# Token-major products of 512 columns in place of pairs of 256, and a ring of 11 small weight pieces in place of two whole blocks

## The chip, the cores and the metric

The kernel runs on one core of one Trainium2 chip. The metric is the device time of one execution in microseconds. Three runs of the kernel before gave 1104.18, 1104.21 and 1106.66 us; the profile was taken from a further execution of 1107.71 us.

## The reference, cut to what matters

Two layers of a streaming encoder over 1024 prompt positions and 8 x 16 sample frames, 1152 rows in all, with a model width of 1024. Per layer:

```python
h = x @ w_in                                   # 1024 -> 3072, split into eleven parts
uA, vA, zA, qB, fB, iB, zB, qC, kC, vC, zC = jnp.split(h, split_pts, axis=-1)
yA = sgu(uA, vA, ...) * silu(zA)               # chunked gMLP gating, mixer A
yB = hgrn2(silu(qB), 1 - f, iB, log f) * silu(zB)   # gated linear recurrence, mixer B
yC = window_attention(rope(qC), rope(kC), vC, sinks) * silu(zC)   # mixer C
out = layer_norm(alpha * x + concat(yA, yB, yC) @ w_out)          # 1024 -> 1024
```

All data is float32. The two large products, `x @ w_in` and `mix @ w_out`, are the bulk of the arithmetic.

## The kernel before, in words

The 1152 rows are nine tiles of 128. A group is three tiles (`GROUPS`); there are three groups per layer and six groups in all, numbered n = 0 to 5. Group n = 1 and n = 4 hold the sample tile.

**Split products.** Each float32 operand is split into a high and a low part (`wh` and `wl` for weights, `xh` and `xl` for the input, `mixh` and `mixl` for the mixers' output), and a product is the sum of three: high x high, low x high, high x low. `prod` issues 24 matmuls for it: eight slices of the depth times three kinds, one kind after the other. In `tok_major` the tile of 128 rows is the stationary operand and the weights stream, 256 columns at a time; in `feat_major` the weights are stationary and the 384 rows of a group stream.

**Weight blocks.** The weights come in blocks of 1024 x 256. A group uses 12 blocks of `w_in` and 4 of `w_out` (of the group before), in the order that the strings `P0`, `PN` and `PL` give; six of the twelve are token-major (K, Q0, Q1, I, ZB, V), as are O0 to O3, and the six others (F, Q, U, Z, C0, C1) are feature-major. A token-major block is three products, one for each tile; a feature-major one is two. Two blocks have room at a time (`wh` and `wl` with two buffers each). `next_w` hands out a block and at once issues the loads of the block after the next one to come.

**Raw and kept blocks.** A block that is used for the first time is loaded raw in four pieces of 256 KB through a staging ring (`wst`, four buffers), and each piece is split: ScalarE copies the high part, VectorE or GpSimd subtracts to get the low one. From the sixth block on (`NFIRST`) both parts are also written to DRAM, and later groups load them from there without splitting: two parts of 1 MB for a block, in DMAs of 512 KB. In group 0 and in group 3 most blocks are split; in group 1 the first five blocks of layer 0 are split again and kept this time, and so are the four of `w_out`.

**Lanes.** The mixers' own work (attention `lane_c`, recurrence `lane_b`, gating `lane_a`) is written as generators. `tick()` advances each of the three lanes by one step after every product; "+C", "+B", "+A" in a plan start a lane, "-C", "-X" and "-BX" run it out to its end. TensorE executes in the order of the program text; the order on the other engines and on SP's DMA queue is made by a list scheduler, in which weights have a high priority.

**Output.** `out_block` runs in the next group's plan, between attention's steps; `out_norm` does the layer norm of a tile after the last of its four blocks. `setup_out` loads the norm's weights once per layer into tiles of their own. After group 5 the four output blocks run with no lanes beside them.

The part of the plan of the middle groups that matters: `K Q0 Q1 -BX +C O0 O1 O2 O3 +X F Q U I +B ZB Z -C C0 C1 +N -X V +A`; of the last group: `K Q0 Q1 -BX +C O0 O1 O2 O3 +X U F Q I +B ZB Z -X V +A -C C0 C1`.

Of the kernel before, what the change touches and what calls it, by code (L numbers as in the profile page):

```python
# [25 lines left out]
TINY = float(2.0 ** -60)  # L26
NWST = 4
WDVE = ((1, 3), (1, 3))
NB1 = 3
NC4 = 3  # L30
PPT = 1
NEA = 3
NFIRST = 5
WDVE0 = (0, 1, 2, 3)
# [13 lines left out]
P0 = 'K Q0 Q1 -BX +C +X I F Q +B ZB U Z -C C0 C1 +N -X V +A'  # L48
PN = 'K Q0 Q1 -BX +C O0 O1 O2 O3 +X F Q U I +B ZB Z -C C0 C1 +N -X V +A'
PL = 'K Q0 Q1 -BX +C O0 O1 O2 O3 +X U F Q I +B ZB Z -X V +A -C C0 C1'  # L50
# [47 lines left out]
def body(ctx: ExitStack, tc: tile.TileContext, A, O, cst):  # L98
# [122 lines left out]
    def setup_out(l):  # L221
        d = lay[l]
        for n, k in (("ln_g", "lng"), ("ln_b", "lnb")):
            d[k] = T(k, [P, D], 1)
            nc.sync.dma_start(d[k], A[n][l].partition_broadcast(P))
# [10 lines left out]
    def setup_a(l):  # L236
        d = lay[l]
        for n, k in (("ln_v_g", "vg"), ("ln_v_b", "vb")):
            d[k] = T(k, [P, 256], 1)
            nc.sync.dma_start(d[k], A[n][l].partition_broadcast(P))  # L240
        d["bs"] = T("bs", [P, 2, P], 1)
        nc.sync.dma_start(d["bs"], A["bs"][l])
        rs = T("wst", [P, 4, 16], NWST)
        acquire("wst", NWST, nc.sync.dma_start(rs.rearrange("p g i -> p (g i)"), A["wss"][l].rearrange("j g i -> j (g i)").unsqueeze(0).to_broadcast([8, 16, 64])))
# [5 lines left out]
        up = tt(pool, wsS.rearrange("p g (c j) -> p g c j", c=8), rs.unsqueeze(2).to_broadcast([P, 4, 8, 16]),  # L250
                C("b8").unsqueeze(1).unsqueeze(3).to_broadcast([P, 4, 8, 16]), ALU.mult)
        release("wst", up)

    def plan(n):
        if n == 0:
# [4 lines left out]
    IN_COLS = {"K": 2304, "Q0": 1792, "Q1": 2048, "F": 1024, "Q": 768, "I": 1280, "ZB": 1536, "V": 256, "C0": 2560,  # L260
               "C1": 2816, "U": 0, "Z": 512}
    wlist = []
    for n, (l, g) in enumerate(order):
        for b in plan(n):
            if b in IN_COLS:
                wlist.append((l, "w_in", IN_COLS[b] // CB))
            elif b[0] == "O":
                wlist.append((order[n - 1][0], "w_out", int(b[1])))
    wlist += [(order[-1][0], "w_out", cb) for cb in range(4)]
    wq = []  # L270
    wpos = [0]
    kept = {}

    pieces = []

    def issue_w(off=WP):
        if wpos[0] >= len(wlist):
            return
        l, name, blk = wlist[wpos[0]]
        first = wpos[0]  # L280
        early = first if first < NEA else None
        eng_lo = WDVE0 if early is not None else WDVE[l]
        wpos[0] += 1
        key = (l, name, blk)
        with tc.high_priority(offset=off):
            wh, wl = T("wh", [P, 8, CB], 2, F32R), T("wl", [P, 8, CB], 2, F32R)
            if key in kept:
                for h in range(2):
                    ks = slice(4 * h, 4 * h + 4)
                    nc.sync.dma_start(wh[:, ks, :].bitcast(F32), kept[key][0][:, ks, :])  # L290
                    nc.sync.dma_start(wl[:, ks, :].bitcast(F32), kept[key][1][:, ks, :])
                wq.append((wh, wl))
                return
            keep = None
            if first >= NFIRST:
                nm = f"{name}{l}_{blk}"
                keep = kept[key] = [dp.tile([P, 8, CB], F32, tag=nm + c, name=nm + c) for c in "hl"]
            for kk in range(4):
                tag, bufs = ("wst", NWST) if early is None or kk == 3 else ("pT", 3) if early % 2 == 0 else ("c4", NC4)
                st = T(tag, [P, 2, CB], bufs)  # L300
                ld = nc.sync.dma_start(st, A[name][l, :, blk, 2 * kk:2 * kk + 2, :])

                def piece(kk=kk, st=st, tag=tag, bufs=bufs, ld=ld):
                    hw, lw = wh[:, 2 * kk:2 * kk + 2, :], wl[:, 2 * kk:2 * kk + 2, :]
                    with tc.high_priority(offset=WP):
                        copy(hw, st)
                        up = tt(dve if kk in eng_lo else pool, lw, st, hw.bitcast(F32), ALU.subtract)
                        if kk % 2 and keep:
                            ks = slice(2 * kk - 2, 2 * kk + 2)
                            nc.scalar.dma_start(keep[0][:, ks, :], wh[:, ks, :].bitcast(F32))  # L310
                            nc.sync.dma_start(keep[1][:, ks, :], wl[:, ks, :].bitcast(F32))
                    acquire(tag, bufs, ld)
                    release(tag, up)
                pieces.append(piece)
        wq.append((wh, wl))

    def do_pieces(k):
        for _ in range(min(k, len(pieces))):
            pieces.pop(0)()

    def next_w():
        do_pieces(99)
        w = wq.pop(0)
        issue_w()
        return w
# [24 lines left out]
    def tick():  # L350
        do_pieces(PPT)
# [3 lines left out]
    def prod(out, lh, ll, rh, rl, wmov, early=False):  # L355
# [4 lines left out]
        else:  # L360
            seq = [(ab, k) for ab in (hh, wh, wl) for k in range(8)]
        for n, ((a, b), k) in enumerate(seq):
            pe.matmul(out, a(k), b(k), start=n == 0, stop=n == 23)  # L363

    def tok_major(w, x, tt_, evac, early=False):
        ps = MM([P, CB])
        prod(ps, lambda k: x[0][:, k, tt_ * P:(tt_ + 1) * P], lambda k: x[1][:, k, tt_ * P:(tt_ + 1) * P],
             lambda k: w[0][:, k, :], lambda k: w[1][:, k, :], True, early)
# [3 lines left out]
    def feat_major(w, x, u, evac):  # L372
        ps = MM([P, 384])
        prod(ps, lambda k: w[0][:, k, u * P:(u + 1) * P], lambda k: w[1][:, k, u * P:(u + 1) * P],
             lambda k: x[0][:, k, :], lambda k: x[1][:, k, :], False)
# [499 lines left out]
    def out_block(op, cb):  # L875
        l, tiles = op["l"], op["tiles"]
        if cb == 0:
            if "lng" not in lay[l]:
                setup_out(l)
            op["ys"] = load_x(l, tiles)  # L880
            op["sts"] = [T("lst", [P, 4, 6], 3) for _ in tiles]
        ys, sts = op["ys"], op["sts"]
        w = next_w()
        cs = slice(cb * CB, (cb + 1) * CB)
        for tl, t in enumerate(tiles):
            def ev(ps):
                dve.scalar_tensor_tensor(ys[tl][:, cs], ys[tl][:, cs], ALPHA, ps, ALU.mult, ALU.add)
                dve.bn_stats(sts[tl][:, cb, :], ys[tl][:, cs])
                if cb == 3:
                    out_norm(l, t, ys[tl], sts[tl], LNM[op["n"]][tl])  # L890
            tok_major(w, mix, tl, ev)

    def out_norm(l, t, y, st, mode):
        d = lay[l]
# [3 lines left out]
        n = {"P": 0, "S": 768}.get(mode, D)  # L898
        if n < D:
            nb = T("sm", [P, 4], 12)  # L900
            dve.scalar_tensor_tensor(nb[:, 0:1], mv[:, 0:1], -1.0, mv[:, 2:3], ALU.mult, ALU.mult)
            z = y[:, n:]
            act.activation(z, z, AF.Identity, scale=mv[:, 2:3], bias=nb[:, 0:1])
            tt(pool, z, z, d["lng"][:, n:], ALU.mult)
            tt(pool, z, z, d["lnb"][:, n:], ALU.add)
        if n > 0:
            z = y[:, 0:n]
            dve.scalar_tensor_tensor(z, z, mv[:, 0:1], d["lng"][:, 0:n], ALU.subtract, ALU.mult)
            if mode == "A":
                act.activation(z, z, AF.Copy, scale=mv[:, 2:3])  # L910
                tt(pool, z, z, d["lnb"], ALU.add)
            else:
                dve.scalar_tensor_tensor(z, z, mv[:, 2:3], d["lnb"][:, 0:n], ALU.mult, ALU.add)
        if mode == "S":
            nc.sync.dma_start(yrows(l, t)[:, 0:n], y[:, 0:n])
            nc.sync.dma_start(yrows(l, t)[:, n:], y[:, n:])
        else:
# [10 lines left out]
    issue_w(2 * WP - 100)  # L928
    with tc.high_priority(offset=2 * WP - 200):
        xrs += load_xT(GROUPS[0][1:])  # L930
    pending, vlast = None, [None]

    def run_group(n, l, g, prev):
# [30 lines left out]
        def qc(qb):  # L964
            qks = G["qks"]
            w = next_w()
            for tl, t in enumerate(tiles):
                def ev(ps):
                    if t == "s":
                        copy(qks[tl][:, 0:8, :].rearrange("p (u r g) d -> p g r u d", u=2, g=2)[:, qb],  # L970
                             ps.rearrange("p (r u d) -> p r u d", r=2, u=2))
                    else:
                        copy(qks[tl][:, 4 * qb:4 * qb + 4, :], ps.rearrange("p (h d) -> p h d", h=4))
                    if qb == 1:
                        rope(l, t, qks[tl])
# [38 lines left out]
        def ib():  # L1014
            G["vts"] = [T("vt", [P, 2, 4, 64], 3) for _ in range(3)]
            w = next_w()
            for tl, t in enumerate(tiles):
                def ev(ps):
                    VS, v = G["vts"][tl], ps.rearrange("p (h v) -> p h v", h=4)
                    if t == "s":  # L1020
                        copy(VS[:, 0], v)
                    else:
                        copy(VS[0:64, 0], v[0:64])
                        copy(VS[64:128, 1], v[64:128])
                tok_major(w, x, tl, ev)
# [3 lines left out]

        def zb_():  # L1030
            w = next_w()
            zb = G["zb"]
            for tl in range(3):
                def ev(ps):
                    silu2(ps, 256, zb[:, tl, :])
                    z4 = zb[:, tl, :].rearrange("p (h v) -> p h v", h=4)
                    tt(eng("f"), z4, z4, d["ng"].unsqueeze(1).to_broadcast([P, 4, 64]), ALU.mult)
                tok_major(w, x, tl, ev)
# [126 lines left out]
```

## Time and profile before

| | |
|---|---|
| median of three runs | 1104.21 us |
| the profiled execution | 1107.71 us |
| its span, first to last instruction | 1105.6 us |
| TensorE busy with matmuls | 1069.6 us, 97% of the span |
| VectorE, ScalarE, GpSimd busy | 664.2, 513.2, 379.1 us |
| bytes moved by DMA | 269 MB, 243 GB/s on average |
| mean granted clock of TensorE | 0.989 of full speed |

Matmuls are pipelined: the duration shown of one is longer than the distance from one to the next, so the distance between the starts of rows in order of time is what a matmul costs. A row "x8" of the timeline merges eight instructions in a row.

### The profile page before, as it was taken

How to read it: one execution, taken by the hardware profiler on the slowest of the kernel's cores; microseconds unless marked ns; L12 is line 12 of the kernel's file. 1: busy time of each engine (PE TensorE's matmuls, PEld its weight loads, DVE VectorE, ACT ScalarE, POOL GpSimd, SP SyncE). 2: the span in 40 equal slices, each digit the busy share in tenths (PEclk: the TensorE clock that was granted, in tenths of full speed). 3: DMA queues.
4: the chain of work that ended last, by engine and by line, in shares of the span. 5: the costliest groups of instructions: out<-in, count | busy, mean ns of one | idle time of the engine just before them, and what ended most of it. 6: DMA issues, size and time to landing. Idle time of an engine off the chain costs nothing. (4 is left out here: it accounts for less than half of the span.)

```text
span 1105.6 us, 25914 instructions
## 1 busy us (share of the span) xinstructions
PE 1069.6 (97%) x10267; PEld 1003.1 (91%) x10267; DVE 664.2 (60%) x1714; ACT 513.2 (46%) x1297; POOL 379.1 (34%) x500
## 2 busy tenths in 40 slices
PE   9988999999999999999999998999999999999996
PEld 7977799998999999999999988999989999999996
DVE  4678654856374466277468678467536726746744
ACT  5687554655332376234257654345443324453310
POOL 3344375233224103384205465151405121123502
PEclk9998999999999999999999998999999999999999
DMA  9574589986558657656947987776856675576463
GB/s 323 186 260 160 185 307 357 307 314 249 181 202 295 217 184 270 226 196 242 345 181 266 349 306 278 274 256 243 297 189 204 216 269 197 186 280 218 161 224 134
DMA packets 88521, 269.07 MB, mean 243 GB/s; under 512 B 10448, under 2 KB 14032, under 8 KB 88400
## 3 DMA queue, kind: packets, MB, share of 16 engines
q1 hardware_dynamic: 79184, 233.86, 61.1%
q10 hardware_dynamic: 9216, 33.56, 7.9%
q8 instruction: 81, 1.33, 0.5%
q14 instruction: 40, 0.33, 0.1%
HBM read 188.73 MB, written 78.64 MB: 242 GB/s over the span
## 5 line engine op out<-in xcount | busy, mean ns | idle before, releaser
L143 POOL TENSOR_TENSOR wl<-wst,wh 128x512 fp32r<-128x512 f32 x68 | 97.8, 1449 | 200.2 <-ACT wh L126 129.4
L363 PE MATMUL mm<-wh,xh 128*128 128x256 f32 x864 | 128.4, 291 | 5.1 <-DVE t3k L383 2.6
L388 POOL TENSOR_TENSOR sm<-sm,ct 128x4 f32<-128x4 f32 (+2 forms) x42 | 47.9, 1141 | 225.3 <-DVE sm L387 225.3
L363 PE MATMUL mm<-wh,xl 128*128 128x256 f32 x864 | 123.3, 285 | 0.5 <-POOL xl L143 0.5
L363 PEld LDWEIGHTS mm<-wh,xh 128*128 128x128 f32 x864 | 111.8, 192 | 11.8 <-ACT wh L126 3.4
L363 PE MATMUL mm<-wl,xh 128*128 128x256 f32 x864 | 122.1, 284 | 0.0
L363 PE MATMUL mm<-xh,wh 128*128 128x384 f32 x576 | 121.2, 353 | 0.7 <-DVE t3k L383 0.7
L363 PEld LDWEIGHTS mm<-wh,xl 128*128 128x128 f32 x864 | 112.9, 194 | 0.7 <-POOL xl L143 0.7
L363 PE MATMUL mm<-xl,wh 128*128 128x384 f32 x576 | 112.5, 336 | 0.0
L363 PEld LDWEIGHTS mm<-wl,xh 128*128 128x128 f32 x864 | 112.4, 193 | 0.0
L363 PE MATMUL mm<-xh,wl 128*128 128x384 f32 x576 | 111.7, 335 | 0.0
L363 PEld LDWEIGHTS mm<-xh,wh 128*128 128x128 f32 x576 | 99.9, 192 | 4.8 <-issue 1.1
L126 ACT ACTIVATE wh<-wst 128x512 fp32r<-128x512 f32 x139 | 81.8, 625 | 44.2 <-DMA wst<-in_w_in 21.7
L363 PEld LDWEIGHTS mm<-xl,wh 128*128 128x128 f32 x576 | 102.2, 190 | 0.0
L143 DVE TENSOR_TENSOR wl<-wst,wh 128x512 fp32r<-128x512 f32 x71 | 70.9, 1007 | 51.1 <-ACT wh L126 46.2
L363 PEld LDWEIGHTS mm<-xh,wl 128*128 128x128 f32 x576 | 100.9, 188 | 0.0
L363 PE MATMUL mm<-wh,mixh 128*128 128x256 f32 x576 | 85.0, 290 | 1.5 <-ACT mixh L126 1.5
L363 PE MATMUL mm<-wh,mixl 128*128 128x256 f32 x576 | 80.8, 283 | 0.0
L363 PE MATMUL mm<-wl,mixh 128*128 128x256 f32 x576 | 80.8, 283 | 0.0
L477 ACT ACTIVATE c<-ax,sm 128x256 f32<-128x256 f32 (+1 forms) x128 | 57.2, 459 | 46.7 <-DVE sm L474 39.3
L363 PEld LDWEIGHTS mm<-wh,mixh 128*128 128x128 f32 x576 | 73.8, 191 | 1.7 <-ACT mixh L126 1.7
L363 PEld LDWEIGHTS mm<-wl,mixh 128*128 128x128 f32 x576 | 74.3, 192 | 0.0
(212 smaller groups left out, 1870.8 us busy)
## 6 DMA issues: line engine op xcount, KB each, us to landing
wst<-in_w_in SPq DMA_DIRECT2D x107, 256.0 KB, 5.5
xrow<-x SPq DMA_DIRECT2D x18, 512.0 KB, 4.5
wst<-in_w_out SPq DMA_DIRECT2D x32, 256.0 KB, 5.2
x<-xrow SPq DMA_DIRECT2D x9, 512.0 KB, 7.2
xrow<-in_xT SPq DMA_DIRECT2D x8, 512.0 KB, 6.7
xrow<-in_x_prompt SPq DMA_DIRECT2D x8, 512.0 KB, 6.0
wh<-w_in_3h SPq DMA_DIRECT2D x8, 512.0 KB, 5.5
wl<-w_in_3l SPq DMA_DIRECT2D x8, 512.0 KB, 7.9
```

The lines of the kernel that those rows point to most:

```text
L126: return act.activation(o, i, AF.Copy)
L143: return e.tensor_tensor(o, a, b, op=op)
L363: pe.matmul(out, a(k), b(k), start=n == 0, stop=n == 23)
L388: pool.tensor_tensor(out, out, mh[:, :out.shape[-1]], op=ALU.pow)
L477: acquire("c4", NC4, *[act.activation(pt[:, h, sl], pss[h // 2][:, h % 2, sl], AF.Exp, bias=nM[:, h:h + 1], scale=0.125, accum_out=rs[:, h ...
```

## The change

**Wide units.** Q0 and Q1 become one unit QC of 512 columns, I and ZB become IZ, and O0 to O3 become two units O0 and O1 of 512 columns. Their products stream 512 columns for each stationary tile. K, V and the feature-major blocks stay as they are. In a wide product there is a `tick()` after the twelfth matmul as well as at its end.

**Order in a product.** The three kinds now alternate for each slice of the depth, in place of one kind after the other.

**Ring.** The weights lie in 11 pieces (`NPC`) of [128, 2, 512]: 512 KB with both parts. A block of 256 columns is four pieces with two slices of the depth each, a wide unit eight pieces with one slice each. When the last product of a unit has made its last use of a piece, the piece is given back (`release`) and `pump` issues the next piece of the list. A kept piece is loaded by two DMAs of 256 KB. All raw pieces go through the four staging buffers; before, most of the first three blocks used other buffers too.

**Plan.** The lane of mixer B now starts after IZ, so ZB no longer stands behind its start.

**Norm.** The norm's weights are loaded for every group, in four tiles of 512 columns from the pool `t3k`, whose five buffers the recurrence's inputs use too. The norm works on halves of 512 columns; in mode "S" (the last group) VectorE does the first half and ScalarE and GpSimd the second, where the cut was at column 768 before.

```diff
+NPC = 11
-NEA = 3
-NFIRST = 5
+NEA = 2
+NFIRST = 4
-PN = 'K Q0 Q1 -BX +C O0 O1 O2 O3 +X F Q U I +B ZB Z -C C0 C1 +N -X V +A'
-PL = 'K Q0 Q1 -BX +C O0 O1 O2 O3 +X U F Q I +B ZB Z -X V +A -C C0 C1'
+PN = 'K QC -BX +C O0 O1 +X F Q IZ +B U Z -C C0 C1 +N -X V +A'
+PL = 'K QC -BX +C O0 O1 +X U F Q IZ +B Z -X V +A -C C0 C1'
...
     def setup_out(l):
-            d[k] = T(k, [P, D], 1)
-            nc.sync.dma_start(d[k], A[n][l].partition_broadcast(P))
+            for h in range(2):
+                r.append(T("t3k", [P, 512], 5))
+                nc.sync.dma_start(r[-1], A[n][l][512 * h:512 * h + 512].partition_broadcast(P))
...
+    def job(u, j):
+        l, name, i = wlist[u]
+        key = (l, name, i)
+        np_ = 4 if name == "w2" else 8
+        if j == 0 and key not in kept and u >= NFIRST:
+            nm = f"{name}{l}_{i}"
+            kept[key] = u, [dp.tile([P, np_, 512], F32, tag=nm + c, name=nm + c) for c in "hl"]
+        src, keep = kept.get(key, (u, None))
+        if src < u:
+            pc = T("w", [P, 2, 512], NPC, F32R)
+            acquire("w", NPC, *[nc.sync.dma_start(pc[:, c, :].bitcast(F32), keep[c][:, j, :]) for c in range(2)])
+        else:
+            st = T("wst", [P, 512], NWST)
+            raw = A[name][l, i].rearrange("p k c -> p (k c)")[:, 512 * j:512 * j + 512]
+            acquire("wst", NWST, nc.sync.dma_start(st, raw))
+            pc = T("w", [P, 2, 512], NPC, F32R)
+            hi = copy(pc[:, 0, :], st)
+            acquire("w", NPC, hi)
+            release("wst", tt(dve if u < NEA or j % 2 else pool, pc[:, 1, :], st, pc[:, 0, :].bitcast(F32), ALU.subtract))
+            if keep:
+                nc.scalar.dma_start(keep[0][:, j, :], pc[:, 0, :].bitcast(F32))
+                nc.sync.dma_start(keep[1][:, j, :], pc[:, 1, :].bitcast(F32))
...
+    def pump(off=WP, upto=1 << 30):
+        while jobs and jobs[0][0] < upto and rings["w"][0] - NPC < len(rings["w"][1]):
+            with tc.high_priority(offset=off):
+                job(*jobs.pop(0))
...
-            seq = [(ab, k) for ab in (hh, wh, wl) for k in range(8)]
+            seq = [(ab, k) for k in range(8) for ab in (hh, wh, wl)]
+        wide = out.shape[-1] == 512
         for n, ((a, b), k) in enumerate(seq):
-            pe.matmul(out, a(k), b(k), start=n == 0, stop=n == 23)
+            mm = pe.matmul(out, a(k), b(k), start=n == 0, stop=n == 23)
+            if per and n % (3 * per) == 3 * per - 1:
+                release("w", mm)
+                pump()
+            if wide and n == 11:
+                tick()
...
     def tok_major(w, x, tt_, evac, early=False):
-        ps = MM([P, CB])
+        n, per = 64 * len(w[0]), 8 // len(w[0]) if tt_ == 2 else None
+        ps = MM([P, n])
```

## Rows read from the trace of the kernel before

**Rows 1.** The page: busy time, and the span in 40 slices, in tenths.

```profile
PE 1069.6 (97%) x10267; PEld 1003.1 (91%) x10267; DVE 664.2 (60%) x1714; ACT 513.2 (46%) x1297; POOL 379.1 (34%) x500
...
PE   9988999999999999999999998999999999999996
...
DMA  9574589986558657656947987776856675576463
```

**Rows 2.** Groups by line and shape, TensorE: count, busy us, mean ns, idle before.

```profile
L363 PE MATMUL mm<-wh,xh 128*128 128x256 f32 x864 | 128.4, 291 | 5.1 <-DVE t3k L383 2.6 <-ACT wh L126 1.9 <-ACT vt L126 0.5
...
L363 PE MATMUL mm<-xh,wh 128*128 128x384 f32 x576 | 121.2, 353 | 0.7 <-DVE t3k L383 0.7
...
L363 PE MATMUL mm<-wh,mixh 128*128 128x256 f32 x576 | 85.0, 290 | 1.5 <-ACT mixh L126 1.5
```

**Rows 3.** Timeline of TensorE, in two stretches of uninterrupted products: start, duration.

```profile
239.71 1.55 PE L363 MATMUL mm<-xh,wh 128*128 128x384 f32 x8
...
242.48 1.55 PE L363 MATMUL mm<-xh,wl 128*128 128x384 f32 x8
...
1084.33 1.12 PE L363 MATMUL mm<-wh,mixh 128*128 128x256 f32 x8
...
1094.89 1.12 PE L363 MATMUL mm<-wl,mixh 128*128 128x256 f32 x8
```

**Rows 4.** Timeline of the TensorE end of group 5: lane B's last steps, first output product.

```profile
1048.58 0.69 PE L829 MATMUL ax<-vt,AQ 128*64 128x64 f32 x16
...
1059.34 0.38 PE L845 MATMUL ax<-idn,t1b 128*128 128x128 f32 x2
...
1062.03 0.39 PE L363 MATMUL mm<-wh,mixh 128*128 128x256 f32 x1 [1.48 <-ACT mixh L126]
```

**Rows 5.** Timeline of all engines: a step of lane B, first and last instruction.

```profile
1033.38 0.69 PE L829 MATMUL ax<-vt,AQ 128*64 128x64 f32 x16
...
1038.74 0.42 DVE L143 TENSOR_TENSOR t1b<-ax,t1b 128x256 f32<-128x256 f32 x1
```

**Rows 6.** Stages: PE, PEld, DVE, ACT, POOL busy (count), clock, DMA share, GB/s.

```profile
155.00:254.00 99.00, 97.51 (x770) 92.96 (x768) 60.59 (x128) 54.31 (x127) 43.49 (x46) 1.00 0.93 328
...
390.00:400.00 10.00, 10.00 (x87) 9.91 (x86) 5.85 (x17) 7.66 (x24) 0.00 (x0) 1.00 0.59 209
590.00:690.00 100.00, 94.17 (x926) 86.42 (x928) 74.85 (x173) 59.07 (x127) 53.37 (x62) 0.97 0.88 314
205.00:235.00 30.00, 30.00 (x250) 27.89 (x249) 24.02 (x53) 18.76 (x54) 8.48 (x6) 1.00 0.81 276
```

**Rows 7.** Timeline of SP's queue, group 2: a kept block's four loads.

```profile
381.98 0.79 SPq L290 DMA_DIRECT2D wh<-w_out_2h  x2
382.94 0.79 SPq L291 DMA_DIRECT2D wl<-w_out_2l  x2
```

**Rows 8.** DMA issues: count, KB each, median us from issue to landing.

```profile
wst<-in_w_in SPq DMA_DIRECT2D x107, 256.0 KB, 5.5
...
wl<-w_out_2l SPq DMA_DIRECT2D x8, 512.0 KB, 7.0
```

**Rows 9.** Groups by line and shape: the splitting of one raw piece.

```profile
L143 POOL TENSOR_TENSOR wl<-wst,wh 128x512 fp32r<-128x512 f32 x68 | 97.8, 1449 | 200.2 <-ACT wh L126 129.4 <-PE mm L363 35.6 <-DVE lst L888 8.4
...
L126 ACT ACTIVATE wh<-wst 128x512 fp32r<-128x512 f32 x139 | 81.8, 625 | 44.2 <-DMA wst<-in_w_in 21.7 <-PE mm L363 13.6 <-DMA wst<-in_w_out 4.1
...
L143 DVE TENSOR_TENSOR wl<-wst,wh 128x512 fp32r<-128x512 f32 x71 | 70.9, 1007 | 51.1 <-ACT wh L126 46.2 <-PE mm L363 3.5 <-POOL X L143 1.1
```

**Rows 10.** Timeline of all engines: the end of the last tile's norm.

```profile
1097.79 0.42 DVE L888 BATCH_NORM_STATS2 lst<-xrow 128x6 f32<-128x256 f32 x1
...
1102.25 0.72 POOL L143 TENSOR_TENSOR xrow<-xrow,lnb 128x256 f32<-128x256 f32 x1
1103.00 0.33 SPq L916 DMA_DIRECT2D out_y_prompt<-xrow  x1
```

**Rows 11.** Timeline of TensorE at the start: first product of the second block.

```profile
18.02 1.21 PE L363 MATMUL mm<-wh,xh 128*128 128x256 f32 x8
```

More of the change, by code (lines that the diff above doesn't have):

```diff
@@ L264, in body @@
         for b in plan(n):
[L265 to L271, printed above, removed]
-    kept = {}
[L274 to L315, printed above, removed]
@@ L317, in do_pieces @@
-    def do_pieces(k):
-        for _ in range(min(k, len(pieces))):
-            pieces.pop(0)()
+            if b in UNITS:
+                wlist.append((order[n - 1][0] if b[0] == "O" else l, *UNITS[b]))
+    wlist += [(order[-1][0], "wo", cb) for cb in range(2)]
+    kept = {}
+    units = [([], []) for _ in wlist]
+    jobs = [(u, j) for u, (_, name, _) in enumerate(wlist) for j in range(4 if name == "w2" else 8)]
+    rings["w"] = [0, []]
+    ucur = [0]
+    def job(u, j):
[20 more added lines that the diff above has]
+                nc.sync.dma_start(keep[1][:, j, :], pc[:, 1, :].bitcast(F32))
+        units[u][0].append(pc[:, 0, :])
+        units[u][1].append(pc[:, 1, :])
@@ L373, in feat_major @@
         ps = MM([P, 384])
-        prod(ps, lambda k: w[0][:, k, u * P:(u + 1) * P], lambda k: w[1][:, k, u * P:(u + 1) * P],
-             lambda k: x[0][:, k, :], lambda k: x[1][:, k, :], False)
+        prod(ps, wcols(w[0], u * P, (u + 1) * P), wcols(w[1], u * P, (u + 1) * P),
+             lambda k: x[0][:, k, :], lambda k: x[1][:, k, :], False, per=2 if u == 1 else None)
         evac(ps)
@@ L877, in out_block @@
         if cb == 0:
-            if "lng" not in lay[l]:
-                setup_out(l)
+            op["ln"] = setup_out(l)
             op["ys"] = load_x(l, tiles)
-            op["sts"] = [T("lst", [P, 4, 6], 3) for _ in tiles]
+            op["sts"] = [T("lst", [P, 2, 6], 3) for _ in tiles]
         ys, sts = op["ys"], op["sts"]
         w = next_w()
-        cs = slice(cb * CB, (cb + 1) * CB)
+        cs = slice(512 * cb, 512 * cb + 512)
         for tl, t in enumerate(tiles):
@@ L897, in out_norm @@
         rstd(mv[:, 2:3], mv[:, 1:2], LN_EPS)
-        n = {"P": 0, "S": 768}.get(mode, D)
-        if n < D:
+        if mode in "PS":
             nb = T("sm", [P, 4], 12)
             dve.scalar_tensor_tensor(nb[:, 0:1], mv[:, 0:1], -1.0, mv[:, 2:3], ALU.mult, ALU.mult)
[L902 to L911, printed above, removed]
-            else:
[L913 to L917, printed above, removed]
+        for h in range(2):
+            g, b, z = ln[0][h], ln[1][h], y[:, 512 * h:512 * h + 512]
+            if mode == "P" or mode == "S" and h == 1:
+                act.activation(z, z, AF.Identity, scale=mv[:, 2:3], bias=nb[:, 0:1])
+                tt(pool, z, z, g, ALU.mult)
+                tt(pool, z, z, b, ALU.add)
+            else:
+                dve.scalar_tensor_tensor(z, z, mv[:, 0:1], g, ALU.subtract, ALU.mult)
+                if mode == "A":
+                    act.activation(z, z, AF.Copy, scale=mv[:, 2:3])
+                    tt(pool, z, z, b, ALU.add)
+                else:
+                    dve.scalar_tensor_tensor(z, z, mv[:, 2:3], b, ALU.mult, ALU.add)
+            if mode == "S":
+                nc.sync.dma_start(yrows(l, t)[:, 512 * h:512 * h + 512], z)
+        if mode != "S":
             nc.sync.dma_start(yrows(l, t), y)
@@ L962, in kv, with qc @@
                 params()
-        def qc(qb):
+        def qc():
             qks = G["qks"]
@@ L1100, in run_group @@
                 "-BX": lambda: drain("B", "X")}
-        for i in range(4):
+        for i in range(2):
             acts[f"O{i}"] = lambda i=i: out_block(prev, i)
@@ L1110, in body @@
     drain("B", "X")
-    for cb in range(4):
+    for cb in range(2):
         out_block(pending, cb)
@@ L1122, in _layout @@
     xs, xp = i["x_sample"].reshape(1, 128, 8, 128), i["x_prompt"].reshape(8, 128, 8, 128)
-    blocks = lambda w: w.reshape(2, 8, 128, -1, CB).transpose(0, 2, 3, 1, 4)
+    cols = lambda w, at, n: np.stack([w.reshape(2, 8, 128, -1)[..., c:c + n] for c in at], 1).transpose(0, 1, 3, 2, 4)
     rows = lambda v: np.broadcast_to(v.reshape(1, -1), (128, v.size))
```

82 lines of the change are left out of this document (39 added, 43 removed).

## The prediction

> **What bounds the kernel now.** I read the busy times first: TensorE has matmuls in flight for 97% of the span, the others far less, and the row of 40 slices is full but for three 8s, the start and the end [rows 1]. So a change of TensorE's own instructions shows in the time, and whatever makes TensorE wait adds to it. But "busy" says nothing of what a matmul costs, since neighbours overlap. I therefore went to the timeline for the distance between starts. With 256 columns, 11 rows of 8 matmuls lie between the starts at 1084.33 and 1094.89: 10.56 us / 88 = 120.0 ns. With 384 columns, two rows of 8 between 239.71 and 242.48: 2.77 us / 16 = 173.1 ns [rows 3]. 128 columns more cost 53.1 ns, which is 2.41 GHz; the rest, 120.0 - 106.2 = 13.8 ns, is paid once per matmul whatever its width. The groups by shape give the counts: three kinds of 864 and three of 576 with 256 columns, 4320 in all, and 1728 with 384 [rows 2]. 4320 x 120.0 + 1728 x 173.1 ns = 817 us, so three quarters of the span are large products. Then the stages: in two long ones, 155 to 254 us (group 1, where weights are split and kept) and 590 to 690 us (group 3), the DMA engines are 93% and 88% busy; elsewhere, as at 390 to 400 us, 59% [rows 6]. DMA is the second thing near its limit, and only there: 328 / 0.93 = 353 GB/s at full load.
>
> **The change, part by part.**
>
> *Width.* Of the 4320 matmuls of 256 columns, those of K and V (2 blocks x 3 tiles x 24 x 6 groups = 864) stay; the 3456 of Q0, Q1, I, ZB and O0 to O3 become 1728 of 512. The trace has none of 512. The lower bound is the line through the two widths: 120.0 + 2 x 53.1 = 226.2 ns. The upper bound is 240.0, two of 256 with nothing saved. I take the line, since 384 columns lie on it together with 256 and nothing in the rows bends there. Gain: 1728 x 13.8 ns = 23.8 us, bounds 0 and 23.8. The stationary operand is loaded before every matmul as now, and the new order within a product changes neither count nor width: 0.
>
> A page speaks against this. The Trainium skill, "TensorE: Matmul & The Clock Gate", section on the back-to-back issue gap, gives N / 2.4 GHz plus about 2.5 ns per matmul, so that a pair would save 2.5 ns: an estimate of 4.3 us in all. The distance of 120.0 ns at 256 columns does not agree with the 109.2 that this gives; I go by the row.
>
> *Steps of the lanes.* A group had 42 ticks: 30 token-major products and 12 feature-major ones. It still has 42: K and V give 6, four wide units of three products give 24, the feature-major ones 12. Twelve wide matmuls last 2.71 us where 24 narrow ones lasted 2.88, so a lane has 0.17 us less between steps: 0, for the slack that TensorE's full row shows, at most some 3 us.
>
> *End of the last group.* Here order costs. Lane B needs twelve steps. Before, ZB, Z, V, C0 and C1 give 12 ticks after its start, and its twelfth step (the transposes at 1059.34) falls on the last tick [rows 4]. Now only Z, V, C0 and C1 follow: 9. Steps 10 to 12 run with no product between them, and TensorE, in order, waits. Step 10's chain, from the matmuls at 1033.38 to the end of the last product on VectorE at 1039.16, took 5.8 us among other work [rows 5], and before it stands the state's update of step 9, which I estimate at a fifth of that, 1.2 us. Against it goes the 1.48 us that the first output product waits now [rows 4], which will be over by then. Upper bound 5.8 + 1.2 - 1.5 = 5.5; lower bound 0, if VectorE and GpSimd have everything ready. I take +3.5, nearer to the row.
>
> *Ring.* In a wide unit 8 of 11 pieces are held, so three of the next unit lie ready. A wide product lasts 24 x 226.2 ns = 5.43 us and uses a piece for 0.68. Piece i is given back 0.68 x (i + 1) us into the last product; its place goes to piece i + 3 of the next unit. If that is wide too, piece 7 is needed 5.43 + 7 x 0.68 = 10.2 us after the last product's start, some 0.7 more with a lane step between. Five pieces, 2.6 MB, have to come in that time. *Kept:* a block's four loads of 512 KB start at 381.98, the last issue is at about 383.4, and it lands 7.0 us later: 2.1 MB in 8.4 us [rows 7, 8]. Half a MB more at 353 GB/s is 1.5 us: 9.9 after the first give-back at 0.68, 10.6 against 10.9. It just fits, and only where nothing else is in the queue. *Raw:* ScalarE needs 0.63 us a piece, VectorE 1.01 or GpSimd 1.45 in turn [rows 9]; four pieces wait in staging, the fifth is loaded after the first is split (0.68 + 0.63 + 1.01), lands 5.5 us later [rows 8] and is split by 9.5. It fits if VectorE is free, but in the output stage of group 1 VectorE is busy 24.0 of 30 us [rows 6]. Wide follows wide at QC to O0 and O0 to O1 in groups 1 to 5, and at the last O0 to O1: 11 times, 7 of them into kept and 4 into raw pieces. Everywhere else a narrow unit stands on one side, with 7 pieces ahead or four uses of 1.04 us and more: 0. For the 7 I take 0.3 us each (0 to 1), for the 4 I take 1 us each (0 to 3): +6, bounds 0 and 19. Behind a late weight load on SP's queue stand only further loads, which are less urgent.
>
> *DMA.* The norm's weights are loaded 24 times 256 KB, before 4 times 512: +4.2 MB, of which 1.05 fall on group 1. In the stage at 93% this costs up to 1.05 MB / 353 GB/s = 3.0 us; and its three wide pairs (QC, O0, O1: 3 x 72 x 13.8 ns = 3.0 us) save nothing if DMA sets the pace. Group 3's stage has two such pairs, 2.0 us. Bounds 0 and 8; I take half, +4. More and smaller DMAs: a pair of issues takes 0.79 us [rows 7], a wide piece needs one pair per 0.68 us in a burst of five, which the moving of the bytes outlasts: 0.
>
> *Norm and tail.* The last matmul ends at 1094.89 + 1.12 = 1096.0, the last statistics at 1098.2, the last issue is at 1103.0 [rows 3, 10]. With a wide last product VectorE has the tile before behind it: two instructions of 512 columns, at most twice 0.42 us each, end 1.7 us after the matmul, not 2.2. GpSimd's two instructions double from 0.72 us to at most 1.44, ScalarE's grows some 0.2: -0.5 + 1.4 + 0.2, +1 rounded, bounds 0 and 2.
>
> *Start.* The second unit's first product begins at 18.02 [rows 11] and its eight pieces now pass four staging buffers. Piece loads follow the splitting of K's pieces, in two rounds of about 7 us (5.5 to land, 0.63 and 1.01 to split) from 7 us on: all there by some 21, needed from 18.0 to 22.8. 0, at most +3.
>
> Sum: -23.8 + 3.5 + 6 + 4 + 1 = -9.3 us. The profiled execution took 1107.7 us for a span of 1105.6, so 1098.4 for its like; it lay 3.5 us above the median, and against the median, 1104.2, the forecast is 1095.
>
> **Rivals.** *The ring is ample*, and DMA hides: for it speaks that TensorE hardly waits for weights today, 1.9 us of idle in the largest group [rows 2], and that 11 pieces are more than the 8 of before. Then 1104.2 - 23.8 + 3.5 + 1 = 1085. *Starvation at wide after wide*: the same arithmetic with 0.3 us of slack at its thinnest. Without the ring's term the sum is -15.3 us, so it decides from 15.3 / 11 = 1.4 us per passage on; at 2.5 us, what one norm load of 1 MB in front costs, it gives 1104.2 - 15.3 + 27.5 = 1116. *VectorE and lanes set the pace* where it is 75 to 80% busy [rows 6]: of the 24 pairs half save nothing, -11.9 + 14.5, 1107. *Width saves nothing*, because a product's fixed part grows with the columns: two widths on one line speak against it; 1104.2 + 14.5 = 1119. By the page's rule it would be 1114; the trace gives that little chance.
>
> **How the numbers follow.** Forecast 0.50 (1088 to 1101), ample ring 0.20 (1080 to 1088), VectorE and lanes 0.11, starvation 0.14, no gain of width 0.05. A measurement of this kernel tells from no change what is over about 0.3%, 3.3 us. Faster takes the first two, 0.70; the third lies within and takes 0.02 of starvation's mild cases, 0.13; slower 0.17. The range runs from 1081, nearly the whole gain of width, to 1112, into starvation; the forecast's own is 1088 to 1101.
>
> **What the profile would show.** Distances of 226 ns between wide matmuls, 8539 matmuls in place of 10267. In group 5 a gap of some 4 us on TensorE between the last product of C1 and the first of O0, ended by the transposes of line 845's like. Small waits for weights at the first product of O0 and O1, in groups 1 and 4 for ScalarE or VectorE, else for DMA. DMA near full in groups 1 and 3. The prediction is wrong if wide matmuls lie 240 ns apart, if the waits for weights at the 11 passages sum to well over 6 us or are missing, or if TensorE's idle time grows in stages without wide units.

## The result, and the profile after

The changed kernel took 1135.45 us (median of 4 runs, 1132.46 to 1139.28): 1.0283 times the kernel before, interval 1.0246 to 1.0320. The forecast was 1095 with a range up to 1112; the kernel became slower, by 31 us. The profiled execution took 1132.46 us for a span of 1130.7.

The page, busy times and slices, as in [rows 1]:

```profile
PE 1067.7 (94%) x8539; PEld 914.2 (81%) x8539; DVE 647.8 (57%) x1666; ACT 517.0 (46%) x1287; POOL 375.9 (33%) x506
...
PE   7969999899999999999999898999999999999986
...
PEclk9979999999999999999999999999999999999989
```

The 1728 matmuls fewer are there, but TensorE's idle time rose from 1105.6 - 1069.6 = 36 us to 1130.7 - 1067.7 = 63 us, and holes and a lower clock show at the start. A measurement of one kernel spreads by some microseconds: the interval above is worth 4 us to each side. So a difference between two edited kernels below is uncertain by some 2 to 7 us.

First, what the width gave: the timeline of TensorE in the last output unit, to compare with [rows 3].

```profile
1095.97 0.61 PE L345 MATMUL mm<-w,mixh 128*128 128x512 f32 x2
...
1106.17 0.62 PE L345 MATMUL mm<-w,mixh 128*128 128x512 f32 x2
```

Between these two starts lie 45 matmuls, three for each 0.68 us: 10.20 us / 45 = 226.7 ns, where the line through the two narrower widths gave 226.2. So 1728 x (240.0 - 226.7) = 23.0 us were saved, as forecast, and about 54 us were lost elsewhere. Where TensorE waits for a result of another engine or for a DMA, by the view of waits (engine, tile and line that wait, releaser: us in total, times, longest):

```profile
PE ax L456 <- DVE qT L145: 10.1, 6, 2.4
PE mm L345 <- DVE t3k L376: 7.5, 2, 5.0
PE mm L345 <- ACT w L128: 5.9, 4, 2.8
PE ax L822 <- POOL vt L741: 5.5, 4, 2.6
PE ax L581 <- DVE c L145: 4.5, 2, 2.3
PE ax L838 <- DVE t1b L145: 4.2, 2, 3.3
PE ax L797 <- DMA X<-in_st: 4.2, 2, 2.8
...
PE mm L345 <- DMA w<-wo_1h: 1.1, 3, 0.8
```

The `ax` rows are steps of lanes B and C, the `mm` rows products. A ring that starves TensorE would fill rows like the last; together with two smaller ones of its kind it comes to 1.6 us. Most of the waits are the lanes' (L456 and L581 are lane C, L797, L822 and L838 lane B). Those on `ACT w` are the start. The row on `t3k` is the first product of IZ, which waits for VectorE's work on Q, 5.0 us in group 0 and 2.5 in group 3; the kernel before had 3.3 us of such waits.

The last group, end of lane B, in TensorE's timeline, as in [rows 4] (L822 and L838 are L829 and L845 there; a bracket is the idle time in front and its releaser):

```profile
1060.04 0.33 PE L822 MATMUL ax<-vt,AQ 128*64 128x64 f32 x2
1063.02 0.85 PE L822 MATMUL ax<-vt,AQ 128*64 128x64 f32 x13 [2.65 <-POOL vt L741]
...
1065.43 0.84 PE L345 MATMUL mm<-xh,w 128*128 128x384 f32 x2
1066.07 0.52 PE L345 MATMUL mm<-xl,w 128*128 128x384 f32 x1
1066.39 0.84 PE L345 MATMUL mm<-xh,w 128*128 128x384 f32 x2
...
1080.54 0.91 PE L822 MATMUL ax<-vt,AQ 128*64 128x64 f32 x14 [1.63 <-POOL vt L741]
1084.73 0.69 PE L838 MATMUL ax<-idn,t1b 128*128 128x128 f32 x2 [3.28 <-DVE t1b L145]
...
1085.64 0.63 PE L345 MATMUL mm<-w,mixl 128*128 128x512 f32 x1
...
1086.92 0.63 PE L345 MATMUL mm<-w,mixl 128*128 128x512 f32 x1
```

Three waits, 7.6 us, on a chain that had none in [rows 4] but the 1.48 at its end; and products that run slowly behind them. The windows say why (start:end, length, busy of PE, PEld, DVE, ACT, POOL, granted clock, DMA share, GB/s):

```profile
1045.30:1060.00 14.70, 14.70 (x204) 13.47 (x199) 12.45 (x38) 3.65 (x7) 10.61 (x18) 1.00 0.42 144
...
1064.50:1068.00 3.50, 3.50 (x12) 3.38 (x12) 2.87 (x9) 1.58 (x4) 0.61 (x2) 0.53 0.92 289
...
1081.40:1088.20 6.80, 3.52 (x11) 2.80 (x10) 1.95 (x6) 0.77 (x2) 1.01 (x1) 0.50 0.23 84
```

By the waits of 2.65 and 3.28 us lie stretches at half the clock, 1.2 GHz: the first begins 1.4 us behind its wait, the second takes its wait in. So a wait can cost more than its own length: O0's first matmuls take nearly twice their time. The mean granted clock of the whole span was 0.989 before and 0.978 after; with a low level of 0.5 that is 2 x 0.011 x 1105.6 = 24 us at half clock before, and 2 x 0.022 x 1130.7 = 50 after.

### The profile page after: what moved, and what is told of

The parts are those of the page before. It is cut to its first block, busy times and chain, and to the rows that moved or that the text cites. A ratio compares the mean times of both kernels' runs of the same rounds, so it can differ in the third digit from the quotient of the medians.

```text
span 1130.7 us, 23131 instructions
## 1 busy us (share of the span) xinstructions
PE 1067.7 (94%) x8539; PEld 914.2 (81%) x8539; DVE 647.8 (57%) x1666; ACT 517.0 (46%) x1287; POOL 375.9 (33%) x506
## 4 chain that ended last, share of the span: by engine, by line
PE 65%; DVE 11%; DMA 9%; issue 6%; ACT 5%; POOL 5%; ACTq 0%; SPq 0%; POOLq 0%; DVEq 0%
PE mm L345 50%; DMA wst<-in_w 4%; PE ax L494 2%; PE ax L456 2%; PE ax L485 2%; DVE W L145 1%; POOL X L145 1%; PE ax L570 1%; DVE X L145 1%; ACT w L128 1%; DVE w L145 1%; DMA X<-in_st 1%; DMA wst<-in_wo 1%; POOL w L145 1%; PE ax L855 1%
## 5 line engine op out<-in xcount | busy, mean ns | idle before, releaser
L345 PE MATMUL mm<-w,xh 128*128 128x256 f32 (+1 forms) x1152 | 306.9, 350 | 13.7 <-DVE t3k L376 7.5
L345 PE MATMUL mm<-xh,w 128*128 128x384 f32 x1152 | 313.0, 343 | 0.9 <-DVE tanh L376 0.8
L345 PEld LDWEIGHTS mm<-w,xh 128*128 128x128 f32 x1152 | 205.6, 196 | 45.3 <-DVE t3k L376 8.0
L345 PEld LDWEIGHTS mm<-xh,w 128*128 128x128 f32 x1152 | 212.5, 190 | 4.5 <-ACT t3k L128 1.2
L345 PE MATMUL mm<-w,xl 128*128 128x256 f32 (+1 forms) x576 | 197.7, 345 | 0.0
L345 PE MATMUL mm<-w,mixh 128*128 128x512 f32 x576 | 195.8, 404 | 1.7 <-DMA w<-wo_1h 1.1
L345 PE MATMUL mm<-xl,w 128*128 128x384 f32 x576 | 194.9, 338 | 0.0
L345 PEld LDWEIGHTS mm<-w,xl 128*128 128x128 f32 x576 | 112.6, 196 | 10.7
L345 PE MATMUL mm<-w,mixl 128*128 128x512 f32 x288 | 112.9, 392 | 0.0
L345 PEld LDWEIGHTS mm<-xl,w 128*128 128x128 f32 x576 | 109.8, 191 | 0.2
L456 PE MATMUL ax<-kT,qT 128*128 128x256 f32 (+1 forms) x256 | 42.9, 301 | 10.5 <-DVE qT L145 10.1
```

The source lines that it names most:

```text
L345: mm = pe.matmul(out, a(k), b(k), start=n == 0, stop=n == 23)
L456: pe.matmul(ps[:, hh, sl], qT[:, hh, 2 * g + j, :], kk, start=hh + c == 0, stop=False)
```

## The experiments

Ratios are to the kernel before, run on the same chip beside each. Theory 1, formed from the rows above: the order of the stages, in which lane B starts later and, in groups 1 to 4, U comes later (the section on the change names only the first; the diff has both), leaves lane steps at places where TensorE must wait for them. Rival: the ring.

### The order of the stages

**Lane B late, in the kernel before.**

```diff
-... I +B ZB ...
+... I ZB +B ...
```

> The kernel before with one edit: lane B starts behind ZB, three ticks later, as far as the changed kernel moved it. Theory 1: this edit alone costs a good part of what the changed kernel lost in the lanes, 1114 to 1130. The prediction's own figure for the last group, 3.5 us, would give 1107 to 1108. Rival (ring starvation, which this kernel cannot have): 1104 to 1108.

Measured: 1132.26 us, 1.0247 [1.0218, 1.0275]. With narrow products and no ring, this shift of three ticks alone costs 26 us, a little more than the theory's range.

**The whole new order, in the kernel before.**

```diff
-PN = '... F Q U I +B ZB Z ...'
+PN = '... F Q I ZB +B U Z ...'
```

(in the first and the last group accordingly)

> The kernel before, with the whole stage order of the changed kernel: in all groups I stands next to ZB, lane B starts behind ZB, U behind that. Theory (the order by itself is the largest term of the loss, 20 to 27 us): 1122 to 1136. Rival (it costs so much only with wide products, and lane B's shift, 26 us alone, is mended by U between): 1105 to 1115.

Measured: 1127.67 us, 1.0201 [1.0177, 1.0225]. U between makes it a little milder, 22 us. The end of its last group, TensorE's timeline:

```profile
1058.79 1.14 PE L829 MATMUL ax<-vt,AQ 128*64 128x64 f32 x13 [2.65 <-POOL vt L748]
...
1076.16 0.91 PE L829 MATMUL ax<-vt,AQ 128*64 128x64 f32 x14 [1.63 <-POOL vt L748]
1080.34 0.69 PE L845 MATMUL ax<-idn,t1b 128*128 128x128 f32 x2 [3.27 <-DVE t1b L143]
...
1082.54 1.91 PE L363 MATMUL mm<-wh,mixl 128*128 128x256 f32 x8
...
1085.95 1.20 PE L363 MATMUL mm<-wh,mixh 128*128 128x256 f32 x8
```

The same three waits, to a hundredth, as in the changed kernel. They belong to the order, not to the width. From C0's first product to O0's, this kernel needs 34.3 us, the changed one 34.4 and the kernel before 20.2. (The last two rows are used at the end.)

**The order alone undone, in the changed kernel.** Lane B starts at the evacuation of IZ's second tile, which is its old tick, in groups 1 to 5; U stands in front of IZ.

```diff
-PN = '... F Q IZ +B U Z ...'
-PL = '... F Q IZ +B Z ...'
+PN = '... F Q U IZ Z ...'
+PL = '... F Q IZ Z ...'
...
+                    if tl == 1 and n > 0:
+                        start_b()
```

> The changed kernel with the order alone undone: lane B starts at the end of IZ's second tile in groups 1 to 5, U stands in front of IZ in groups 1 to 4; staging and splits as changed. Theory (order and staging are separate terms; the run with staging too took 1102.5, and staging alone gained 10.6): 1108 to 1117. Rival (with the start late the order's gain is partly lost): 1118 to 1126.

Measured: 1107.81 us, 1.0021 [1.0008, 1.0034]: 27.6 us back. The profiled execution, the slowest of ten, took 1112.35 us. By the starts of the units it is 9.4 us shorter than the changed kernel's in group 5, 6.8 in group 1, 5.5 in group 3 and 2.0 behind group 5; groups 2 and 4 are 3.4 and 1.7 us longer. The same two steps of lane B in the last group:

```profile
1056.09 0.69 PE L822 MATMUL ax<-vt,AQ 128*64 128x64 f32 x16
1066.85 0.38 PE L838 MATMUL ax<-idn,t1b 128*128 128x128 f32 x2
```

No bracket is left. The middle groups show a second form of it. Lane B's sample step is issued at one tick and its state loaded by a DMA, which the next tick's step reads. The load's issue and the first matmul that reads it, in group 1, first in the changed kernel:

```profile
342.89 0.33 SPq L747 DMA_DIRECT2D X<-in_st  x1
...
349.53 0.94 PE L797 MATMUL ax<-X,AQ 64*32 64x64 f32 x64 [2.81 <-DMA X<-in_st]
```

and with the order undone:

```profile
334.13 0.33 SPq L747 DMA_DIRECT2D X<-in_st  x1
...
339.19 0.95 PE L797 MATMUL ax<-X,AQ 64*32 64x64 f32 x64
```

With the new order the second of these ticks is V's first, a product of 24 x 120.0 ns = 2.9 us, and TensorE is there 3.83 us after the issue; with the old one it is C1's second, 24 x 173.1 ns = 4.2 us, and comes after 5.06. The shorter product is the smaller part of it: the load itself took 6.5 us to land in the changed kernel, where the DMA engines are 99% busy from 340 to 350 us, and 4.3 us with the order undone, where they are 67% busy from 333 to 340 us. A load of 4.3 us would have left a wait of 0.5 us and not 2.81. The waits on qT are not of the order: they were 10.1 us in the changed kernel and are 10.2 here. The part on ScalarE's queue is about them.

**Lane B early in all groups, U left behind.** The same start of lane B, in group 0 too, without U's move:

```diff
-... IZ +B U Z ...
+... IZ U Z ...
...
+                    if tl == 1:
+                        start_b()
```

> The changed kernel, with lane B started at the end of the second tile of IZ, which is the tick at which the kernel before starts it (one tick into ZB), and nothing else moved. Theory 1 (lane B's late start is most of the loss: its steps fall into V, C1 and the last C0 and C1, where TensorE waits for its chains and then runs at the low clock): those units return to their times before, about 19 us in groups 0 to 4 and 10 in group 5, so 1105 to 1117. Rival (the ring of weight pieces starves TensorE): the place of lane B changes nothing, 1131 to 1139. Second rival (lane steps at half products squeeze lane C whatever lane B does): lane B and lane C now meet in IZ and U, half of it is lost again, 1118 to 1128.

Measured: 1124.55 us, 1.0164 [1.0138, 1.0190], the second rival's figure. By the starts of the units, group 5 fell from 180.8 to 171.4 us, but group 0 rose from 161.8 to 169.3, and IZ in groups 1 and 4 took 35.8 and 35.7 us, after 32.7 and 31.3. The reading is that lane C's sample steps, which U's two ticks no longer bring forward, meet lane B there; the next run tries it.

**U in front of IZ as well.** With lane B early in groups 1 to 5 and the staging of the next part:

```diff
-PN = '... F Q IZ U Z ...'
+PN = '... F Q U IZ Z ...'
```

> The run with all three edits, with two differences: raw loads again issued with their splits (that edit gained nothing), and U in front of IZ in groups 1 to 4, where the kernel before has it. Theory (lane C's sample steps of groups 1 and 4, which U's two ticks used to bring forward, now meet lane B in IZ: IZ and U together took 47 us there against 44.6 and 40.8 before): these two groups lose 4 to 6 us each, 1100 to 1107. Rival (the order of U makes no difference, the waits only move): 1110 to 1118.

Measured: 1102.50 us, 0.9970 [0.9955, 0.9986], as the theory said; IZ in groups 1 and 4 fell from 35.5 and 35.4 to 29.8 us. The run that this one is compared with had lane B's start and the staging alike, U behind IZ, and the raw loads issued ahead (the edit stands further below):

> The changed kernel with three edits: the staging of the first five pieces of QC in pT and c4, raw loads issued ahead of their splits, and lane B started at the end of the second tile of IZ in groups 1 to 5 (group 0 keeps the late start, which was 7.5 us shorter there). If the causes are separate, the gains add up: 10.6 for the staging, 11 and 7.5 for lane B, 6 to 14 for the raw loads less some 4 that the staging has already: 1095 to 1107. Rival (a stall that is removed only moves on to the next late step): 1108 to 1118.

Measured: 1113.79 us, 1.0073 [1.0051, 1.0095], the rival's figure: the gains did not add up. The long IZ of the early lane B without U's move is one reason. That U's place alone is worth the 11.3 us between the two runs is not shown: they differ in the raw loads too, and in the profiled executions (the slowest of ten with U in front, one of the fastest of ten without) groups 1 and 4 as a whole are only 4.6 and 0.8 us shorter with U in front.

### The start

**Other staging.** The first five raw pieces of QC go through buffers that are idle then.

```diff
-            st = T("wst", [P, 512], NWST)
+            tag, bufs = ("pT", 3) if u == 1 and j < 3 else ("c4", NC4) if u == 1 and j < 5 else ("wst", NWST)
+            st = T(tag, [P, 512], bufs)
```

> The changed kernel, with the first five raw pieces of QC staged in the idle buffers of pT and c4 and not in the ring of four. Theory 3 (the start is late because the raw loads of QC wait for a staging buffer): QC of group 0 goes from 22.3 us to 17 or 18, the whole to 1129 to 1132. Rival (the queues, not the buffers, set when these pieces land): QC stays above 21 and the whole at 1133 to 1138.

Measured: 1124.81 us, 1.0157 [1.0130, 1.0184], 10.6 us less, more than the theory had. In the changed kernel the later loads of QC are issued on SP's queue, and TensorE waits in QC's first tile, as these rows of the timeline show:

```profile
16.79 0.38 SPq L289 DMA_DIRECT2D wst<-in_w  x1
...
18.25 2.74 SPq L289 DMA_DIRECT2D wst<-in_w  x3
...
24.89 0.50 PE L345 MATMUL mm<-w,xh 128*128 128x512 f32 x1 [2.84 <-ACT w L128]
...
26.87 0.80 PE L345 MATMUL mm<-w,xh 128*128 128x512 f32 x1 [0.77 <-ACT w L128]
```

With more staging five of them are out by 9 us:

```profile
6.03 0.65 SPq L290 DMA_DIRECT2D pT<-in_w  x1
...
7.87 0.52 SPq L290 DMA_DIRECT2D c<-in_w  x1
8.53 0.36 SPq L290 DMA_DIRECT2D pT<-in_w  x1
```

QC, from its first product to F's, fell from 22.3 to 17.2 us. With the order undone the same edit gains 1107.81 - 1102.50 = 5.3 us; there F takes back 4.8 of the 7.6 us that QC gains.

### The ring

**9 pieces for 11**, in the changed kernel and, later, in the fastest kernel below:

```diff
-NPC = 11
+NPC = 9
```

> The changed kernel with 9 pieces in the ring of weights and not 11. Theory 1 (the ring costs only the few microseconds at wide products behind wide ones): each of these passages has 1.4 us less lead, some ten of them feel it, 1142 to 1152. Rival (starvation is the bulk of the loss, some 30 us at 11 pieces): two pieces fewer add as much again or more, 1160 and above.

Measured: 1161.26 us, 1.0511 [1.0462, 1.0561], 26 us more: above the theory's range and just at the rival's figure. But the rival's ground, starvation at 11 pieces, is not there in the waits: those for weights behind the start were 1.9 us with 11 pieces.

> The fastest kernel so far (order undone, staging, output weights split off ScalarE) with 9 pieces in the ring. Theory (the ring's price is separate: two pieces fewer cost the changed kernel 26 us in waits for weights at wide units): 1113 to 1124. Rival (part of those waits only met TensorE because raw pieces came late from ScalarE): 1102 to 1112.

Measured: 1131.11 us, 1.0232 [1.0195, 1.0268], 36 us more than with 11, beyond both. The waits of TensorE in this kernel, the larger rows of weights:

```profile
PE mm L346 <- DVE w L145: 6.3, 8, 1.4
...
PE mm L346 <- DMA w<-wo_0h: 2.8, 11, 0.8
PE mm L346 <- POOL w L292: 2.7, 3, 1.1
PE mm L346 <- ACT w L128: 2.5, 3, 1.3
PE mm L346 <- DMA w<-wo_0l: 2.0, 2, 1.3
PE mm L346 <- DMA w<-wo_1h: 1.9, 11, 0.2
PE mm L346 <- DMA w<-w_0h: 1.7, 5, 0.9
```

This is what starvation looks like. With 11 pieces it is absent: of these rows the same kernel then has 2.2 us for ACT w (the start), 0.3 for DVE w and 0.3 for one DMA. Eleven pieces do, as the prediction's arithmetic had it, and two fewer cost more than the whole width gives. No run has 10 or 12.

### ScalarE's queue

The section on the change does not say that the splits moved too. Before, `tick` split one raw piece, and what was left of a block was split when the block was handed out. Now the split of a piece is written when a piece of the ring is given back, within the last product of a unit.

**Raw loads ahead of their splits.** The load is issued when a staging buffer is free, not with its split.

```diff
+            if u > 0:
+                load_ahead()
```

> The changed kernel, with the load of a raw piece issued as soon as a staging buffer is free, and not only when its split is written out; all else as it was. Theory 4 (a split is now written together with its load, so ScalarE waits for the load with lane C's copies of qT queued behind it, and TensorE waits for qT): the four waits on qT in the output products of groups 1 and 4 (7.1 us) and those of group 0 go, 1121 to 1129. Rival (lane steps at half products leave lane C's chain too little time, whatever ScalarE's queue holds): these waits stay, 1131 to 1139.

Measured: 1132.69 us, 1.0234 [1.0209, 1.0259]; the waits on qT stayed (1.55, 1.66 and 0.88 us in group 1). That theory fell; the 2.8 us between the two medians lie within their intervals.

**The output weights' splits off ScalarE**, on top of the order and the staging:

```diff
-            hi = copy(pc[:, 0, :], st)
+            hi = pool.tensor_copy(pc[:, 0, :], st) if name == "wo" else copy(pc[:, 0, :], st)
...
-dve if u < NEA or j % 2 else pool
+dve if u < NEA or j % 2 or name == "wo" else pool
```

> As the run with U in front of IZ, and the raw pieces of the output weights are split by GpSimd (high part) and VectorE (low part), not by ScalarE. Theory (the eight pieces of a wide unit are split in one burst, as the last tile gives them back, and lane C's copies of qT stand behind the burst on ScalarE): the waits on qT in the output products of groups 1 and 4 go, 2 to 3 us in each, 4 to 6 in all. Rival (the lane's own chain is too long for the ticks at half products): the waits stay, within 2 us, or VectorE's added work makes it slower.

Measured: 1094.95 us, 0.9910 [0.9885, 0.9935]: 7.6 us less, more than the theory had, and 0.9% faster than the kernel before. TensorE's waits on qT, without the edit and with it:

```profile
PE ax L457 <- DVE qT L145: 14.2, 6, 3.9
...
PE ax L457 <- DVE qT L145: 7.6, 3, 3.2
```

In groups 1 and 4 they fell from 7.3 to 1.3 us; the rest is group 0's. Without this edit, ScalarE's and TensorE's timeline in group 4's output products:

```profile
749.58 0.64 ACT L128 ACTIVATE w<-wst 128x512 fp32r<-128x512 f32 x1
750.68 0.48 ACT L471 ACTIVATE c<-ax,sm 128x256 f32<-128x256 f32 x1 [0.47 <-DVE sm L468]
...
751.15 0.62 ACT L128 ACTIVATE w<-wst 128x512 fp32r<-128x512 f32 x1
...
753.56 0.59 ACT L128 ACTIVATE qT<-ax 64x512 fp32r<-64x512 f32 x1
...
756.23 0.50 PE L457 MATMUL ax<-kT,qT 128*128 128x256 f32 x2 [2.36 <-DVE qT L145]
```

The splits (`w<-wst`) stand among lane C's softmax (`c<-ax,sm`) on ScalarE, and its copy of qT comes last. It ends at 754.15; VectorE's part of qT follows only at 755.48, behind other work of VectorE, and TensorE waits for that. So VectorE's queue has a share in this wait.

**The same edit in the kernel before**, where the splits have their old places:

```diff
-                        copy(hw, st)
+                        pool.tensor_copy(hw, st) if name == "w_out" else copy(hw, st)
```

> The kernel before, with its output weights split by GpSimd and VectorE and not by ScalarE, one piece per tick as it was. Theory (the burst of eight splits behind a wide unit is what delayed lane C on ScalarE): here the pieces come one per tick, TensorE waits only 0.6 to 1.0 us for these copies, so the same edit gains at most 2 us: 1102 to 1108. Rival (ScalarE is overloaded in these groups whatever the order): it gains as much as it did behind the wide products, 1097 to 1101.

Measured: 1106.14 us, 1.0009 [0.9997, 1.0020]. Nothing to gain there: ScalarE's load as such does not hurt. What differs can be seen in ScalarE's timeline in group 4 of the kernel before:

```profile
749.80 0.59 ACT L126 ACTIVATE qT<-ax 64x512 fp32r<-64x512 f32 x1 [0.45 <-DVE qT L143]
...
753.26 1.66 ACT L126 ACTIVATE wh<-wst 128x512 fp32r<-128x512 f32 x3
```

Here, too, three splits stand in a row, and not one per tick as the expectation had it, but they stand behind the copy of qT and the softmax. So the new places of the splits are the likely cause; that it is a burst of eight is argued, not shown.

**QC's and IZ's raw pieces too** (those of eight pieces, behind the first four units):

```diff
-... if name == "wo" else ...
+... if np_ == 8 and u >= NFIRST else ...
```

> As the run that took the output weights' splits off ScalarE, with the wide input pieces (QC and IZ) of the raw passes behind the first four units taken off it as well. Theory (a burst costs only where lane C's first steps stand behind it, which is O0 and O1): nothing more to gain, QC and IZ have no wait on ScalarE there, 1092 to 1099. Rival (any burst on ScalarE costs): 3 to 6 us less again in groups 1 and 3.

Measured: 1098.63 us, 0.9943 [0.9925, 0.9961]: nothing more.

### Two that moved nothing

**IZ as two passes of 256 columns** over the same eight pieces:

```diff
-... IZ ...
+... I +B ZB ...
```

> As the run with all three edits, but IZ is computed as two passes of 256 columns over the same eight pieces, with lane B started between them in all six groups. It gives back 5.8 us of the width (0.96 us in each of 6 groups). Theory (the wide evacuation of IZ in one lump is what holds up lanes B and C in groups 1 and 4, where IZ with the early lane B took 35.8 us against 32.0 and 30.5 before): these two groups regain 8 us and more, group 0 loses some by the early start: 1096 to 1108. Rival (the lump is no cause): 1103 to 1115, above the run with all three edits by 5 or more.

Measured: 1115.33 us, 1.0088 [1.0060, 1.0117], 1.5 us above the run with all three edits, where the rival had 5 or more; but IZ still takes 34.4 and 35.9 us in groups 1 and 4, so the lump of the wide evacuation does not explain its length.

**IZ first in group 0:**

```diff
-P0 = '... +X F Q IZ +B U Z ...'
+P0 = '... +X IZ F Q +B U Z ...'
...
```

> As the run with U in front of IZ, and in group 0 IZ stands in front of F and Q, where the kernel before has I; lane B starts behind Q there. Theory (in group 0 IZ waits for VectorE's tail of Q and then runs its products at the low clock, 6 us over their nominal time): 3 to 6 us less in group 0 than that run. Rival (group 0 is bound by the lanes' and the splits' work on VectorE and ScalarE, so the order of its products matters little): within 2 us of it.

Measured: 1103.66 us, 0.9973 [0.9951, 0.9994], within 2 us of its counterpart, as the rival said.

## Why the prediction was wrong

The measured time lies above the forecast and above every rival's figure.

- *Width*, -23.8: right, 23.0 by the rows. By the formula that the Trainium skill, "TensorE: Matmul & The Clock Gate", section "Back-to-back issue gap", gives for the isolated gap, a wide matmul would take 512 / 2.4 + 2.5 = 216 ns, an estimate; the trace says 226.7.
- *Steps of the lanes*, 0, and *End of the last group*, +3.5: these failed. The 42 ticks were counted, but not who gets them. Lane B's later start was priced as one overhang in one group, and U's place was not priced at all. The two together cost 22 us put into the kernel before and 27.6 taken out of the changed one. Even in the last group the figure was too small: three waits of 7.6 us and two stretches at half clock, where one chain was counted; C0 and C1 there took 34.4 us after 20.2, and 20.3 with the order undone. Part of these 14 us is lane B's own work, which moved there; the group as a whole grew from 173.1 to 180.8 us, though its width saves 3.8. The step went by the length of a chain "among other work", and did not ask which product's length covers each hand-over. The gap that it looked for at the first product of O0 is there, 3.28 us, but it is one of three. And one of its signs of being wrong came true: TensorE's idle time grew in units without wide products, as in C0 and C1 here and in V of group 1.
- *Start*, 0, at most +3: mis-sized. The loads that were reckoned to be there by 21 us were partly issued only at 18.25 and later; 10.6 us alone, 5.3 behind the order.
- *Ring*, +6, bounds 0 and 19: within its bounds, but some 4 us too large; its waits come to 1.9 us. The steep edge is real, 26 and 36 us for two pieces. Its rival, starvation, takes 2.5 us for a norm load of 1 MB, where the term on DMA has 3.0; with 3.0 its figure would be 1122 and not 1116.
- *VectorE and lanes* is the one rival that names the lanes, but by another mechanism: half the width's gain lost to VectorE's load, 1107, where it was the order of lane steps. The gain from taking splits off ScalarE, 7.6 us, is in no step.
- *Clock*: the prediction priced waits by their length. They also pulled products down to half speed; the 0.97 of one stage in [rows 6] was a sign of it that was not used.
- *Tail*, +1: the last matmul starts at 1120.62 and lasts 0.39, which leaves 9.7 us to the end of the span, after 1105.6 - 1096.0 = 9.6 before: no change. *DMA*, +4: the 4 MB more are there, 273 after 269, but no run tells their price apart.

The sum as the runs have it: -23.0 + 27.6 + 5.3 + 7.6 = 17.5 of the 31 us. The gains of the edits were measured one on top of the other, each with the uncertainty named above. The remaining 14 are not settled. The fastest kernel, too, is 11.5 us faster where 23.0 were to be had. By the starts of the units in its profiled execution, the slowest of seven, its groups 0, 2 and 4 took 154.9, 176.9 and 186.4 us after 151.5, 175.8 and 183.9 before, although the wide products in them should save 1.9, 3.8 and 3.8. Three parts of the change were never taken back alone: the steps of the lanes at half products, the norm's weights in the buffers of `t3k`, and the buffers of `c4`, two after three before.

## What to carry to other kernels

When an order of stages is changed for one reason (here, to pair blocks), follow each interleaved lane through its new ticks: which product lies between a step and the one that needs its result, and is it longer than that chain or than the load that the step started, at the DMA traffic of that stage. A moved start of a lane cost here as much as wide products gave. Try the order alone in the old kernel first: that one run would have shown 22 of the 31 us.

## What was unexpected of the hardware

At half clock the fixed part of a matmul disappears. In the rows of the last group above, three matmuls of 384 columns lie between 1065.43 and 1066.39, 320 ns each, which is 384 / 1.2 GHz; three of 512 between 1085.64 and 1086.92, 426.7 ns each, 512 / 1.2 GHz; at full clock the three widths lie 13.8 to 14.3 ns over columns / 2.41 GHz. In the kernel before with the new order, sixteen matmuls of 256 columns lie between 1082.54 and 1085.95, behind its wait of 3.27 us, at a granted clock of 0.50: 213 ns each, 256 / 1.2 GHz. The Trainium skill, "TensorE: Matmul & The Clock Gate", section "Wait — 56ns, not 53.3ns?", has it so for the low clock, and there the trace agrees. By the two widths, 2 x 213 and 427 ns, wide products save nothing in such stretches. And the low clock outlasts its wait: after the wait of 3.28 us it held until 1088.2, 3.5 us after the wait's end.
